# A diffusion backbone's opening in another order, with six smaller edits along its length

## The chip, the core and the metric

The kernel runs on one core of one Trainium2 chip. That core has a matrix engine (PE, whose weight loads the profile shows as PEld), a vector engine (DVE), an activation engine (ACT), a general engine (POOL), and the SP engine, which here only issues DMA. Matrix products accumulate in eight banks of PSUM, 512 columns of 32 bits each; all other tiles lie in SBUF. The metric is the device time of one execution in microseconds (us), the median over runs. Three runs of the kernel before took 2201.84, 2202.66 and 2203.73 us.

## The reference

Two layers of a hybrid backbone over 512 latent tokens and 256 context tokens, width 1024, all in 32-bit floats. Each layer does this:

```
m  = silu(cond) @ ada_w + ada_b          # six vectors per stream: shift, scale, gate, twice
h  = rms_norm(x) * norm_g * (1 + scale) + shift
u  = h @ w_in                            # one projection: keys, values, queries, pool columns, gate logits
A  = (mean over windows 2,4,8,16 of u_pool - u_pool) @ pool_w * pool_scale
B  = neighbourhood attention (4 heads, 8 x 16 window, bias na_rpb, plus all context keys)
C  = windowed attention with sinks;  D = latent attention with low-rank queries and keys
x += gate1 * (sum_i sigmoid(logits_i) * (branch_i @ w_branch_i)) @ w_out
x += gate2 * swiglu(rms_norm(x) * norm_g2 * (1 + scale2) + shift2)
```

The context tokens use the same weights with their own modulation vectors. In the second layer they give keys and values only. A last `rms_norm` gives the output. The modulation of layer 0 stands before everything else, because `h` needs its shift and scale.

## The kernel before

**Numbers.** A product of two 32-bit matrices is made of three fast ones: each operand is split into a high part (rounded by a copy on ACT, `act_copy` L142) and a low part (the difference, by DVE or POOL), and `mm3` (L148) adds high x high, low x high and high x low. `split_w` (L154) does so for weights; the low part goes to the engine named in `cur["lo"]`. A whole 32-bit product is also possible; the chip runs it as two PE instructions.

**Order of the work.** `Stream` (L36) holds a queue of jobs. A job has a load part, which issues the weights' DMAs and their split, and a run part. When a job starts, the next job's load part is traced too, so weights come one job ahead. A run part yields after each few products with the time it thinks they take, and small pieces of work can be deferred by such a time (`st.defer`) or asked for at once (`st.need`). `drive` feeds jobs between the steps of an attention. Instructions on PE, DVE, ACT and POOL are then placed in each engine's queue by a planner, which goes by the traced order and by its own estimate of when each is ready; SP alone keeps the traced order. A tile's tag has a fixed number of buffers, so an instruction that fills a buffer waits for the last reader of what it held. Raw weights have three such buffers, split ones four. PSUM has three banks under the tag `mm`, two under `sc`, two under `tr` and one under `pv`.

**Opening of layer 0.** SP issues x (twelve tiles), then 32 tiles of 256 KB of the first modulation: four groups of eight (shift and scale for chunks 0 to 3, then for 4 to 7). `ada_start` (L309) runs them as steps: the 16 of the first two groups are whole 32-bit products with the two conditioning columns `cs32`; the other 16 are split, with four columns `csp` (two high, two low), their high part by ACT or, each fourth, by DVE, and their low part by DVE (L328). `ada_run(n)` advances n yields, ten to a group. Meanwhile x is transposed chunk by chunk (`turn_xn` L606). `start_h` (L614) makes one chunk of `h`: for the 512 latent and 256 context columns DVE scales (L617), ACT adds the shift and rounds (L620), DVE makes the low part (L621). Chunks 0 to 3 follow the second group.

**First stage of layer 0**, in `mix` (L1312). First come the token-major rows (`tm_jobs` L656: values and small keys, eight jobs, one for each chunk of `h`, with six accumulators of 416 columns in six banks); the first four jobs alternate with the rest of the modulation. Then the mask load and the biases for the first two heads (`na_bias` L1013: a load and three adds each on POOL), chunks 4 to 7 of `h`, two jobs of pool columns (`pool_job` L716), the first queries (`na_q_job` L993, split by `split_q` L973) and the first keys (L1002, split by `split_k` L959). Each of these three kinds runs all eight chunks for the latent columns and then for the context columns, and leaves its accumulator by a post: the pool post copies it by ACT, adds shifted copies on DVE (L753), and defers a small product with `pool_w` by 20 us. Then neighbourhood attention starts; gate jobs (`gate_job` L798) and the next queries fill its waits. The rows go through DRAM (`vst`) to become attention's values. SP also stores x to DRAM (`xst`, eight stores), after the rows.

**First stage of layer 1.** The mask and the biases come first, then pool columns, first queries, the rows, the first keys, and attention.

**Seams later on.** `side_on` (L1426) and `side_one` (L1434) are jobs without a load part and without products. The first stands ahead of the fourth branch's gate jobs, the second ahead of the output projection; the latter loads the last two chunks of x and finishes two groups of the later modulation. That modulation (`ada_rest` L362) loads its own weights through SP while the products run. In the output projection and the last feed-forward product, `project_jobs` (L1444) runs the latent columns of all blocks before the context columns of the last four, defers `stats` by 2.0 us and `apply` by 5.5 us: sums of squares by PE, a Newton iteration on DVE (`newton` L439), `rstd_diag` (L475) with one diagonal matrix of 128 x 128 for each 128 tokens on DVE (L484), then their spread over rows by PE and the next `h`, chunk by chunk.

**The end.** `final_jobs` (L1607) adds the last products to x, squares on ACT, joins the halves' sums, runs `newton_col` (L455) on one column and scales the rows.

## Time and profile before

| what | value |
|---|---|
| median of three runs | 2202.66 us |
| lowest and highest | 2201.84, 2203.73 us |
| time of the profiled execution | 2204.7 us |
| its span, first to last instruction | 2202.9 us |
| mean granted clock of PE | 0.99 |
| busy: PE, DVE, ACT, POOL | 2136.4, 1252.0, 878.2, 715.4 us |

All rows come from the one profiled execution. Times in them count from the start of its span. "Busy" is the time in which an engine has an instruction under way; matrix products are pipelined, so their lengths overlap. An instruction is named by its line, engine and operation, then by what it writes and reads (`out<-in`) and the shapes. What stands in brackets is the time its engine was idle before it and what ended that. The granted clock is 1.00 at 2.4 GHz and 0.50 at 1.2 GHz; a value between is a mean over the stretch.

### The profile page before, as it was taken

Reading aid. Unit: us, or ns where it says so; the run is one execution under the profiler, and the core shown is the slowest. Engines: PE = TensorE matmul, PEld = TensorE weight load, DVE = VectorE, ACT = ScalarE, POOL = GpSimd, SP = SyncE. Lnnn points to the kernel's source line nnn. Section 1 sums busy time; section 2 is a strip of 40 time slices with the busy share of each in tenths; the row PEclk is TensorE's granted clock in tenths of the full one; section 3 lists DMA queues with packets and bytes.
Section 4 is the critical chain, followed back from the end, with each engine's and each line's share of the span. In section 5 each row is a group of like instructions: output and inputs, shape, how many; then the busy total and the mean of one; then the engine's idle time right before and its main releaser. Section 6 shows DMA issues by size and latency. Waiting matters only on the chain.

```text
span 2202.9 us, 32481 instructions
## 1 busy us (share of the span) xinstructions
PE 2136.4 (97%) x11796; PEld 1835.6 (83%) x11796; DVE 1252.0 (57%) x2804; ACT 878.2 (40%) x1967; POOL 715.4 (32%) x593
## 2 busy tenths in 40 slices
PE   7999999999999999999999989999999999999998
PEld 3888888888887898888888868887878898888886
DVE  6764667866799797555522264667776435212225
ACT  4454455544422322122122324555655434323233
POOL 1232222222223233333233322433233343444443
PEclk9999999999999999999999999999999999999999
DMA  7522122111356154444422223322222332333332
GB/s 253 155 73 53 44 51 53 42 41 51 121 174 188 48 168 138 139 143 152 142 66 62 87 79 92 99 66 63 57 68 66 91 111 82 100 96 93 105 96 91
DMA packets 316373, 214.74 MB, mean 97 GB/s; under 512 B 17434, under 2 KB 281908, under 8 KB 316212
## 3 DMA queue, kind: packets, MB, share of 16 engines
q1 hardware_dynamic: 307796, 204.79, 32.0%
q10 hardware_dynamic: 8416, 7.87, 1.1%
q8 instruction: 93, 1.52, 0.3%
q14 instruction: 68, 0.56, 0.1%
HBM read 202.90 MB, written 9.70 MB: 97 GB/s over the span
## 4 chain that ended last, share of the span: by engine, by line
PE 86%; DVE 6%; ACT 2%; issue 2%; DMA 2%; POOL 1%; SPq 0%; ACTq 0%; DVEq 0%; POOLq 0%
PE ps_w L149 13%; PE ps_w L150 13%; PE ps_w L151 13%; PE ps_gate L149 6%; PE ps_gate L150 6%; PE ps_gate L151 6%; PE pv L885 3%; PE tr L871 2%; PE ps_wo L151 2%; PE ps_wo L149 2%; PE ps_wo L150 2%; PE ps_y L149 2%; PE ps_y L151 1%; PE ps_y L150 1%; PE sc L934 1%
## 5 line engine op out<-in xcount | busy, mean ns | idle before, releaser
L157 POOL TENSOR_TENSOR gatelo<-gater,gatehi 128x512 fp32r<-128x512 f32 x128 | 172.9, 1353 | 427.9 <-ACT gatehi L143 412.6
L149 PE MATMUL ps_gate<-hh,gatehi 128*128 128x512 f32 (+1 forms) x768 | 277.9, 362 | 0.0
L150 PE MATMUL ps_gate<-hl,gatehi 128*128 128x512 f32 (+1 forms) x768 | 273.4, 356 | 0.0
L151 PE MATMUL ps_gate<-hh,gatelo 128*128 128x512 f32 (+1 forms) x768 | 272.9, 355 | 0.0
L400 DVE SCALAR_TENSOR_TENSOR adaacc<-adaraw,cs,adaacc 128x512 f32<-128x512 f32 x224 | 160.5, 749 | 86.1 <-DMA adaraw<-in_ada_w_dram 85.0
L149 PE MATMUL ps_w<-hh,w1hi 128*128 128x512 f32 (+1 forms) x480 | 170.8, 356 | 0.0
L149 PE MATMUL ps_w<-hh,w3hi 128*128 128x512 f32 (+1 forms) x480 | 170.3, 355 | 0.0
L150 PE MATMUL ps_w<-hl,w1hi 128*128 128x512 f32 (+1 forms) x480 | 170.0, 354 | 0.0
L150 PE MATMUL ps_w<-hl,w3hi 128*128 128x512 f32 (+1 forms) x480 | 170.0, 354 | 0.0
L151 PE MATMUL ps_w<-hh,w1lo 128*128 128x512 f32 (+1 forms) x480 | 169.8, 354 | 0.0
L151 PE MATMUL ps_w<-hh,w3lo 128*128 128x512 f32 (+1 forms) x480 | 169.8, 354 | 0.0
L157 POOL TENSOR_TENSOR w1lo<-w1r,w1hi 128x512 fp32r<-128x512 f32 x80 | 103.8, 1298 | 198.8 <-ACT w1hi L143 196.8
L149 PE MATMUL ps_w<-gh,w2hi 128*128 128x512 f32 (+1 forms) x472 | 165.6, 351 | 0.0
L151 PE MATMUL ps_w<-gh,w2lo 128*128 128x512 f32 (+1 forms) x472 | 165.4, 350 | 0.0
L150 PE MATMUL ps_w<-gl,w2hi 128*128 128x512 f32 (+1 forms) x472 | 165.2, 350 | 0.0
L157 POOL TENSOR_TENSOR w3lo<-w3r,w3hi 128x512 fp32r<-128x512 f32 x80 | 105.4, 1324 | 178.7 <-ACT w3hi L143 164.7
L151 PEld LDWEIGHTS ps_gate<-hh,gatelo 128*128 128x128 f32 x768 | 145.1, 189 | 19.7
L149 PEld LDWEIGHTS ps_gate<-hh,gatehi 128*128 128x128 f32 x768 | 145.3, 189 | 17.5
L150 PEld LDWEIGHTS ps_gate<-hl,gatehi 128*128 128x128 f32 x768 | 145.4, 189 | 16.6
L157 POOL TENSOR_TENSOR w2lo<-w2r,w2hi 128x512 fp32r<-128x512 f32 (+1 forms) x80 | 97.4, 1225 | 158.0 <-ACT w2hi L143 156.5
L1510 DVE SCALAR_TENSOR_TENSOR ft<-ft,ps_w 128x512 f32<-128x512 f32 (+1 forms) x68 | 39.6, 582 | 143.8 <-ACT ft L1509 143.6
L143 ACT ACTIVATE gatehi<-gater 128x512 fp32r<-128x512 f32 x128 | 80.3, 630 | 81.7 <-PE ps_gate L150 39.9
(419 smaller groups left out, 5599.2 us busy)
## 6 DMA issues: line engine op xcount, KB each, us to landing
adaraw<-in_ada_w_dram SPq DMA_DIRECT2D x160, 256.0 KB, 4.0
gater<-in_w_in_dram SPq DMA_DIRECT2D x128, 256.0 KB, 2.8
w1r<-in_ffn_w_dram SPq DMA_DIRECT2D x80, 256.0 KB, 2.9
w3r<-in_ffn_w_dram SPq DMA_DIRECT2D x80, 256.0 KB, 2.9
w2r<-in_ffn_w_dram SPq DMA_DIRECT2D x56, 256.0 KB, 2.8
ada<-in_ada_w_dram SPq DMA_DIRECT2D x32, 256.0 KB, 5.4
wbr<-in_w_branch_dram SPq DMA_DIRECT2D x64, 128.0 KB, 2.5
wor<-in_w_out_dram SPq DMA_DIRECT2D x32, 256.0 KB, 3.7
```

Source lines behind the costliest of these rows:

```text
L143: nc.scalar.activation(out=o, in_=i, func=AF.Copy, scale=scale)
L149: nc.tensor.matmul(ps, ah, bh, start=start, stop=False)
L150: nc.tensor.matmul(ps, ah, bl, start=False, stop=False)
L151: return nc.tensor.matmul(ps, al, bh, start=False, stop=stop).ins
L157: cur["lo"].tensor_tensor(out=lo, in0=raw, in1=hi.bitcast(F32), op=ALU.subtract)
L400: nc.vector.scalar_tensor_tensor(out=acc[j], in0=raw, scalar=c, in1=acc[j], op0=ALU.mult, op1=ALU.add)
L871: nc.tensor.transpose(tr[:, 128 * j:128 * j + 128], ps[qi][0][:, c0:c0 + 128], ident)
L885: nc.tensor.matmul(acc[:, 128 * q0:128 * (q0 + nq)], v[rows], t[rows, c:c + 128 * nq], start=(i == 0), stop=(i == nmm - 1))
L934: nc.tensor.matmul(ps, q[:, c0:c0 + 128], kd[:, k0:k0 + n], start=True, stop=False)
L1510: nc.vector.scalar_tensor_tensor(out=t, in0=t, scalar=1.0, in1=p1, op0=ALU.add, op1=ALU.mult)
```

## The change

It has seven parts. (1) The modulation steps of the first four groups alternate: even ones are whole, odd ones are split; ACT makes every high part; the low parts of the first two groups go to POOL, those of the last two to DVE. (2) Layer 0's first stage starts with both pool columns and the first queries together, as two jobs: chunks 0 to 3 of all three, then chunks 4 to 7; then come the rows, then the keys. The three raw weight tiles that SP loads among the first modulation weights belong to them. (3) The mask load, the stores of x and the biases of the first two heads move behind the opening or the rows, the biases in layer 1 too; a gate job asks for the pool columns after its first product. (4) The rows' six accumulators take their banks in another order. (5) `newton` leaves its result in SBUF, and the diagonals are made by ACT. (6) The jobs `side_on` and `side_one` go; the latter's work runs at the start of the first block of the output projection, and `apply` is deferred by 8.0 us there in layer 0. (7) At the end one instruction scales and joins the halves' sums.

```diff
-    cs32 = cp.tile([128, KD, 2], F32, name="cs32")
+    cs32 = cp.tile([128, KD, 4], F32, name="cs32")
...
-        nc.vector.tensor_copy(cs32, src)
+        nc.vector.memset(cs32[:, :, 2:4], 0.0)
+        nc.vector.tensor_copy(cs32[:, :, 0:2], src)
...
-            raw = ada0[i]
-            if i < 16:
-                w[i] = raw
-                return
-            w[i] = [rp.tile([128, 512], F32R, tag=t, name="ada" + t, bufs=3) for t in ("ph", "pl")]
-            if i % 4 == 3:
-                nc.vector.tensor_copy(w[i][0], raw)
-            else:
-                act_copy(w[i][0], raw)
-            nc.vector.tensor_tensor(out=w[i][1], in0=raw, in1=w[i][0].bitcast(F32), op=ALU.subtract)
-        for i in range(4):
+            raw = w[i] = ada0[i]
+            if i % 2:
+                hi, lo = w[i] = [rp.tile([128, 512], F32R, tag=t, name="ada" + t, bufs=3) for t in ("ph", "pl")]
+                act_copy(hi, raw)
+                (nc.gpsimd if i < 16 else nc.vector).tensor_tensor(out=lo, in0=raw, in1=hi.bitcast(F32), op=ALU.subtract)
+        for i in range(5):
...
-            if n == 2:
-                nc.tensor.matmul(ps[0:2, :], cs32[:, k, :], wi, start=(k == 0), stop=(k == KD - 1))
+            if i % 2 == 0:
+                nc.tensor.matmul(ps[0:4, :], cs32[:, k, :], wi, start=(k == 0), stop=(k == KD - 1))
...
-        g = t
+        g, res = t, y
...
-            V.scalar_tensor_tensor(out=y, in0=t, scalar=1.5, in1=y, op0=ALU.add, op1=ALU.mult)
-        return y
+            V.scalar_tensor_tensor(out=res if i == 2 else y, in0=t, scalar=1.5, in1=y, op0=ALU.add, op1=ALU.mult)
+        return res
...
-            i = nc.vector.tensor_scalar(out=dg[:, 128 * t:128 * t + 128], in0=ident, scalar1=r[:, 2 * t:2 * t + 1], scalar2=None, op0=ALU.mult)
+            i = nc.scalar.activation(out=dg[:, 128 * t:128 * t + 128], in_=ident, func=AF.Copy, scale=r[:, 2 * t:2 * t + 1])
...
+    OPEN = (O_POOL, O_POOL + 128, O_NA_Q)
+    open0 = []
+    def open_raw(i):
+        raw = wp.tile([128, 4, 128], F32, tag="wraw", name="openr", bufs=3)
+        r0, c0 = 512 * (i // 3), OPEN[i % 3]
+        nc.sync.dma_start(raw, a["w_in"][0][r0:r0 + 512, c0:c0 + 128].rearrange("(k p) c -> p k c", p=128))
+        return raw
...
         if i in (13, 15, 17):
-            raw = wp.tile([128, 416], F32, tag="wraw", name="tmr", bufs=3)
-            load_tm(raw, 0, len(tm0))
-            tm0.append(raw)
+            open0.append(open_raw(len(open0)))
...
-                    ps.extend(psum(("mm", "mm", "mm", "sc", "sc", "tr" if last else "pv")[t], "ps_tm", 416) for t in range(6))
+                    ps.extend(psum(tag, "ps_tm", 416) for tag in ("tr", "mm", "mm", "sc", "mm", "sc"))
...
                 if i == 0 and m == 0:
-                    st.need("pool0", "pool1", "xst")
+                    st.need("xst")
...
                     yield from mm_piece(pg, w[0], cur["h"], (s0, s1))
+                    if i == 0 and m == 0:
+                        st.need("pool0", "pool1")
...
+        def opening_jobs(ys):
+            posts = [pool_job(i, ys)[1] for i in range(2)]
+            q, ps = [], []
+            def post_q(p_, piece):
+                if not q:
+                    q.extend(new_q())
+                split_q(p_, piece, q, True)
+            posts.append(post_q)
+            def load(half):
+                out = []
+                for i in range(3):
+                    raw = open_raw(3 + i) if half else open0[i]
+                    tiles = [big("y", [128, 4, 128], F32R, "open" + t) for t in ("hi", "lo")] if i < 2 else None
+                    out.append(split_w(raw, [128, 4, 128], "open", tiles))
+                return out
+            def product(i, k, w):
+                for p_, (s0, s1) in zip(ps[i], (PL, PC)):
+                    hh, hl = cur["h"][k]
+                    cur["pe"] = mm3(p_, w[i][0][:, k % 4, :], w[i][1][:, k % 4, :], hh[:, s0:s1], hl[:, s0:s1], k == 0, k == KD - 1)
+            def run(half, w):
+                if half == 0:
+                    ps.extend((psum("mm", "ps_open"), psum(tag, "ps_open", 256)) for tag in ("sc", "sc", "pv"))
+                for k in range(4 * half, 4 + 2 * half):
+                    for i in range(3):
+                        product(i, k, w)
+                    yield 9 * NT / 2400
+                if half:
+                    for i in range(3):
+                        for k in (6, 7):
+                            product(i, k, w)
+                        for p_, piece in zip(ps[i], (PL, PC)):
+                            posts[i](p_, piece)
+                        yield 6 * NT / 2400
+            return [st.add(lambda w, h=h: run(h, w), lambda h=h: load(h)) for h in range(2)][1], q
...
             def first_biases():
-                nc.sync.dma_start(nam, a["k_namask"])
                 bias.extend(na_bias(e, nam) for e in range(2))
             def after_tm():
...
-                if not last:
-                    for k in range(KD):
-                        st.defer(2.0 + 4.0 * k, lambda k=k: nc.sync.dma_start(xst[k], xn[k]), "xst")
             if not last:
                 cur["lo"] = nc.vector
+                jo, q0 = opening_jobs(y_pool)
                 tm = tm_jobs()
+                jk, k0 = na_k_job(0)
                 for k in range(4):
-                    ada_run((6, 7, 7, 0)[k])
-                    st.until(tm[k], False)
-                nam = big("c", [128, 3, 32, 8], F32, "nam")
-                first_biases()
+                    ada_run(5)
+                    st.step()
                 for k in range(4, KD):
                     start_h(k)
-                jobs = pool_jobs(y_pool)
-                jq0, q0 = na_q_job(0)
-                jk, k0 = na_k_job(0)
+                st.until(jo, False)
+                nam = big("c", [128, 3, 32, 8], F32, "nam")
+                nc.sync.dma_start(nam, a["k_namask"])
+                for k in range(KD):
+                    st.defer(4.0 + 3.0 * k, lambda k=k: nc.sync.dma_start(xst[k], xn[k]), "xst")
                 st.until(tm[-1], False)
                 after_tm()
-                st.until(jobs[1], False)
             else:
                 nam = big("c", [128, 3, 32, 8], F32, "nam")
-                first_biases()
+                nc.sync.dma_start(nam, a["k_namask"])
...
             jq1, q1 = na_q_job(1)
+            first_biases()
             st.until(jk, False)
...
-        def side_on(_):
-            return
-            yield
-        st.add(side_on)
...
-        def side_one(_):
+        def last_turns():
             turn_x(KD - 2)
             st.defer(6.0, lambda: turn_x(KD - 1), "x")
             if not last:
                 ada_until(2)
-            return
-            yield
-        st.add(side_one)
...
+                if b == 16 and m == 0:
+                    last_turns()
...
-                    st.defer(5.5, apply, "norm")
+                    st.defer(8.0 if b == 16 and not last else 5.5, apply, "norm")
...
-                    o = 8 if i else 2 * t + j
+                    o = 2 * t + j + i
                     nc.scalar.activation(out=p[:, c], in_=x[:, c], func=AF.Square, accum_out=ssq[:, o:o + 1])
-                if len(parts) > 1:
-                    nc.vector.tensor_tensor(out=ssq[:, 7:8], in0=ssq[:, 7:8], in1=ssq[:, 8:9], op=ALU.add)
+                    if j:
+                        v = ssq[:, o:o + 1]
+                        nc.vector.tensor_scalar(out=v, in0=v, scalar1=1.0 / D, scalar2=ssq[:, o - 1:o], op0=ALU.mult, op1=ALU.add)
...
-                v = ssq[:, 2 * t + 1:2 * t + 2]
-                nc.vector.scalar_tensor_tensor(out=v, in0=v, scalar=1.0 / D, in1=ssq[:, 2 * t:2 * t + 1], op0=ALU.mult, op1=ALU.add)
-                r = newton_col(v)
+                o = 2 * t + 1 + t // 3
+                r = newton_col(ssq[:, o:o + 1])
```

## Rows read from the trace of the kernel before

**Rows 1.** The page, part 1: busy us, share of the span, instructions.

```profile
PE 2136.4 (97%) x11796; PEld 1835.6 (83%) x11796; DVE 1252.0 (57%) x2804; ACT 878.2 (40%) x1967; POOL 715.4 (32%) x593
```

**Rows 2.** Busy time by stretch: length, PE, PEld, DVE, ACT, POOL, clock, DMA share.

```profile
16.00:33.00 17.00, 17.00 (x52) 3.98 (x50) 6.06 (x23) 2.88 (x6) 0.00 (x0) 1.00 0.99 338
33.00:71.00 38.00, 32.00 (x146) 22.48 (x145) 34.85 (x72) 20.46 (x38) 6.39 (x6) 0.96 0.38 119
114.00:131.00 17.00, 12.46 (x55) 9.92 (x54) 10.02 (x27) 10.72 (x26) 4.13 (x4) 0.80 0.26 64
16.00:131.00 115.00, 103.97 (x487) 74.84 (x486) 79.94 (x191) 52.83 (x107) 21.89 (x18) 0.96 0.55 172
```

**Rows 3.** Chain of waits, 16 to 62 us: start, length, what.

```profile
16.19 6.96 PE ps_ada L341 x16
57.37 0.24 PE ps_ada L343
```

**Rows 4.** DVE groups by line, 33 to 71 us: busy, mean ns, idle before.

```profile
L328 DVE TENSOR_TENSOR adapl<-ada,adaph 128x512 fp32r<-128x512 f32 x16 | 12.7, 823 | 0.1
L617 DVE SCALAR_TENSOR_TENSOR nh<-xn,mod,rrow 128x512 f32<-128x512 f32 (+1 forms) x16 | 9.3, 614 | 0.1
L621 DVE SCALAR_TENSOR_TENSOR hl<-nh,mod,hh 128x512 fp32r<-128x512 f32 (+1 forms) x15 | 8.8, 623 | 0.0
L157 DVE TENSOR_TENSOR tmlo<-tmr,tmhi 128x416 fp32r<-128x416 f32 x5 | 2.9, 582 | 0.0
L325 DVE CAST adaph<-ada 128x512 fp32r<-128x512 f32 x4 | 2.1, 524 | 0.0
L600 DVE TENSOR_SCALAR dg<-ident,nwy 128x128 f32<-128x128 f32 x6 | 1.4, 280 | 0.0
```

**Rows 5.** Timeline of DVE in the opening: start, length, instruction.

```profile
34.54 0.69 DVE L328 TENSOR_TENSOR adapl<-ada,adaph 128x512 fp32r<-128x512 f32 x1
54.49 3.04 DVE L328 TENSOR_TENSOR adapl<-ada,adaph 128x512 fp32r<-128x512 f32 x3
```

**Rows 6.** Timeline of POOL in the opening.

```profile
49.99 6.39 POOL L1024 TENSOR_TENSOR bias<-braw,nam 128x192 f32<-128x192 f32 x6 [48.68 <-DMA braw<-in_k_rpb_dram]
```

**Rows 7.** Busy time by stretch, seams of layer 1.

```profile
1335.00:1345.00 10.00, 8.11 (x35) 7.61 (x35) 3.31 (x9) 2.52 (x5) 2.20 (x3) 0.83 0.18 47
1380.00:1385.00 5.00, 2.98 (x16) 2.11 (x16) 4.79 (x13) 2.93 (x9) 2.67 (x3) 1.00 0.46 112
```

**Rows 8.** Timeline of the SP queue before the output projection.

```profile
655.12 10.59 SPq L373 DMA_DIRECT2D adaraw<-in_ada_w_dram  x6
665.80 0.94 SPq L163 DMA_DIRECT2D wor<-in_w_out_dram  x2
```

**Rows 9.** Busy time by stretch, start of the output projection, layer 0.

```profile
665.00:680.00 15.00, 10.84 (x45) 8.43 (x44) 13.05 (x22) 3.73 (x7) 5.53 (x4) 0.77 0.80 238
```

**Rows 10.** Busy time by stretch, start of the output projection, layer 1.

```profile
1775.00:1785.00 10.00, 7.94 (x51) 7.53 (x51) 2.32 (x3) 3.21 (x6) 4.76 (x4) 0.83 0.38 109
```

**Rows 11.** Timeline: diagonals on DVE, and a 128 x 128 pass on ACT.

```profile
736.42 3.02 DVE L484 TENSOR_SCALAR dg<-ident,ps_ssq 128x128 f32<-128x128 f32 x4
...
104.73 0.30 ACT L143 ACTIVATE pwh<-pwr 128x128 fp32r<-128x128 f32 x1
```

**Rows 12.** Busy time by stretch, second norm of layer 0.

```profile
735.00:745.00 10.00, 7.96 (x49) 7.28 (x48) 8.17 (x15) 4.36 (x9) 5.14 (x4) 0.83 0.52 160
```

**Rows 13.** Timeline of DVE at the end.

```profile
2195.47 1.13 DVE L1655 SCALAR_TENSOR_TENSOR ssq<-ssq 128x1 f32<-128x1 f32 x1
```

**Rows 14.** Timeline: first pool add, last query split, and PE after it.

```profile
88.13 2.42 DVE L753 TENSOR_TENSOR pb<-pb 128x527 f32<-128x527 f32 x2 [4.45 <-ACT pb L143]
...
112.27 0.43 DVE L984 SCALAR_TENSOR_TENSOR q<-ps_naq,q 64x256 fp32r<-64x256 f32 x1
...
118.76 0.38 PE L149 MATMUL ps_pw<-yph,pwh 128*128 128x256 f32 x1 [3.89 <-DVE ypl L779]
```

More of the change, by code (lines that the diff above doesn't have):

```diff
@@ L333, in ada_start @@
         for i, (b0, k) in enumerate(steps):
-            prepare(i + 4)
+            prepare(i + 5)
             if k == 0:
                 ps = psum("tr", "ps_ada")
-            wi = w.pop(i)
-            n = 2 if i < 16 else 4
-            if n == 2:
-                nc.tensor.matmul(ps[0:2, :], cs32[:, k, :], wi, start=(k == 0), stop=(k == KD - 1))
+            wi = w[i]
+            if i % 2 == 0:
+                nc.tensor.matmul(ps[0:4, :], cs32[:, k, :], wi, start=(k == 0), stop=(k == KD - 1))
             else:
@@ L346, in ada_start @@
             if k == KD - 1:
-                row = tmp([n, 512], F32, "adar")
-                act_copy(row, ps[0:n, :])
+                row = tmp([4, 512], F32, "adar")
+                act_copy(row, ps[0:4, :])
                 yield
-                ps2 = psum("tr", "ps_adat", 4 * n)
+                ps2 = psum("tr", "ps_adat", 16)
                 for j in range(4):
-                    nc.tensor.transpose(ps2[:, n * j:n * j + n], row[:, 128 * j:128 * j + 128], ident[:n, :n])
-                if n == 2:
-                    ada_cols(0, b0, ps2.rearrange("p (j c) -> p j c", c=2), 2)
-                    yield
-                    continue
+                    nc.tensor.transpose(ps2[:, 4 * j:4 * j + 4], row[:, 128 * j:128 * j + 128], ident[:4, :4])
                 red = cp.tile([128, 4, 2], F32, tag="adared", name="adared", bufs=1)
@@ L448, in newton @@
         V.tensor_scalar(out=y.bitcast(I32), in0=g.bitcast(I32), scalar1=-1, scalar2=0x5F3759DF, op0=ALU.mult, op1=ALU.add)
-        for _ in range(3):
+        for i in range(3):
             V.scalar_tensor_tensor(out=t, in0=y, scalar=-0.5, in1=v, op0=ALU.mult, op1=ALU.mult)
             V.tensor_tensor(out=t, in0=t, in1=y, op=ALU.mult)
-            V.scalar_tensor_tensor(out=y, in0=t, scalar=1.5, in1=y, op0=ALU.add, op1=ALU.mult)
-        return y
+            V.scalar_tensor_tensor(out=res if i == 2 else y, in0=t, scalar=1.5, in1=y, op0=ALU.add, op1=ALU.mult)
+        return res
     def newton_col(v):
@@ L540, in transposed @@
         return ps
-    tm0 = []
+    OPEN = (O_POOL, O_POOL + 128, O_NA_Q)
[5 more added lines that the diff above has]
+        return raw
     def load_tm(raw, l, k):
@@ L659, in load @@
             def load(k):
-                if l == 0 and k < len(tm0):
-                    raw = tm0[k]
-                else:
-                    raw = wp.tile([128, 416], F32, tag="wraw", name="tmr", bufs=3)
-                    load_tm(raw, l, k)
+                raw = wp.tile([128, 416], F32, tag="wraw", name="tmr", bufs=3)
+                load_tm(raw, l, k)
                 return split_w(raw, [128, 416], "tm")
@@ L1309, in mla_heads @@
             return heads
+        def opening_jobs(ys):
[25 more added lines that the diff above has]
+                if half:
+                    for i in range(3):
+                        for k in (6, 7):
[4 more added lines that the diff above has]
+            return [st.add(lambda w, h=h: run(h, w), lambda h=h: load(h)) for h in range(2)][1], q
         def mix():
@@ L1438, in side_one @@
                 ada_until(2)
-            return
-            yield
-        st.add(side_one)
         def project_jobs(w, name, h_, b, new_norm, first, rest, r0=0, kn=KD):
```

## The prediction

> **What bounds the kernel now.** I read the page's busy times first, then busy time by stretch, then groups by line, the chain and the timeline where PE stood idle. PE is busy for 97% of the span [rows 1], so only its idle and slow-clocked time can be won back, or an end that no PE work covers. By stretch, 16 to 131 us holds 103.97 us of PE busy in 115 at a mean granted clock of 0.96 [rows 2]: 11.0 us idle, and 0.04 x 115 = 4.6 us lost to the lower of its two levels (1.2 instead of 2.4 GHz), 15.6 in all. From 16 to 33 PE is full and the DMA share is 0.99. From 33 to 71 DVE is the bound: 34.85 of 38 us. From 114 to 131 PE stands 4.5 us and loses 0.20 x 17 = 3.4 to the clock [rows 2]: the first attention waits for keys and pooled columns. Small holes of the same kind lie at 665, 735, 1335, 1380 and 1775 us, and the end is a serial DVE chain.
>
> **The modulation steps.** A whole step is two PE instructions: sixteen of them take 6.96 us, 0.87 a step. A split step is two of 0.24, 0.48 [rows 3]. Before, 16 steps are whole and then 16 split; after, each pair has one of each. PE's total is unchanged, 8 x 0.39 = 3.1 us of it moves from the first two groups to the last two. The wider stationary operand (4 columns, two of zeros) I cost at nothing: the split steps already use 4 columns at 0.24. DVE keeps 8 of 16 low parts and no copy. Eight low parts go to POOL, idle from 16 to 33 [rows 2]; ACT makes all 16 high parts, with 2.9 of 17 us used there.
>
> **DVE in 33 to 71.** Its load now: low parts 12.7, the scaled chunks 9.3 and 8.8, token-major low parts 2.9, copies 2.1, diagonals 1.4 [rows 4]. Low parts cost 0.69 alone, but 3.04 for three while POOL adds the biases from 49.99 for 6.39 us [rows 5, 6]. Those adds leave this stretch. After: 8 x 0.69 = 5.5 (7.2 less), no copies (2.1 less), and for five token-major splits the six of 512 columns, 6 x 0.69 = 4.1 (1.2 more): 34.85 - 8.1 = 26.8 us. Beside it PE has 8 x 0.87 + 8 x 0.48 = 10.8 us of modulation and four chunks of the opening, each 9 x 0.24 + 9 x 0.12 = 3.2 us, 12.9 together. With 23.7 us against 26.8 the two nearly match; chunks 4 to 7 then come at some 2.4 us each from DVE (9.3 + 8.8 for 7.75 chunks [rows 4]) against 3.2 us of PE. PE becomes the bound.
>
> **The new order.** Pooled columns, first queries, token-major rows and first keys are the same PE work. Their posts (pool chains, query split) now run under eight token-major chunks instead of beside first attention. SP issues three 256 KB loads early instead of three times three small ones, three more after the late rows' loads, then the token-major ones; the eight stores of x now go out in that stage. I cost these issues at nothing, since PE has the first half to run; if SP is held up there, the second half is late by that. The pool need, moved behind the first gate product, removes a wait; the mask load is covered by the same stage. Layer 1 of the kernel already runs pool, queries, rows, keys in this order, so it prices the seams: entering the rows it loses 10 - 8.11 = 1.9 idle and 0.17 x 10 = 1.7 clock, and entering attention 2.0 idle at full clock [rows 7]. Left over of the 15.6: 2.0 for attention, 1.8 (half of 3.6, because the one bank that waits for the query split is now asked for fifth and not third), and 2 for the first two groups, which now run at the pace of landing weights, since DMA is already full there [rows 2]. The opening gains 15.6 - 5.8 = 9.8 (bounds: 0 and 15.6). The same bank order gains 0.7 at layer 1's rows (0 to 3.6).
>
> **The stub before the output projection.** SP issues its first weights at 665.80 because it first sat in the six modulation loads queued at 655.12, for 10.59 us [rows 8]. Without the stub they are issued one gate job earlier, ahead of those loads, with some ten us to land and be split. The stretch 665 to 680 loses 15 - 10.84 = 4.2 idle and 0.23 x 15 = 3.5 clock [rows 9]. Next late is the last merged chunk, used eighth by the first product. I take 6.5 of 7.6 (bounds 0 to 7.6). In layer 1 the same seam loses 10 - 7.94 = 2.1 and 1.7 [rows 10]; its weights do land in time and PE waits for a merged chunk that ACT takes behind a weight copy. With SP's order changed I take 1.5 (0 to 3.8). The other stub I cost at nothing: no hole stands there.
>
> **Diagonals on ACT.** At 736.42 four cost DVE 3.02 us; a 128 x 128 pass costs ACT 0.30 [rows 11], so 1.2. But this edit also sends the normalisation 2.5 us later down PE's stream, so its chunks start about when they do now. Of the 10 - 7.96 = 2.0 idle and 1.7 clock there [rows 12] I take 1.0 (0 to 3.7). Elsewhere (queries' and keys' norms, layer 1's first norm) DVE is freed of the same work: 1.1 together, an estimate from 0.75 a piece under POOL (0 to 3). Behind ACT's new passes wait its exponentials, by 0.6 to 1.2 us, under PE work.
>
> By the Trainium skill, SBUF — State Buffer, section "SBUF: two separate sides", DVE with a two-port mode or two SBUF inputs and a reading GpSimd lock each other out for a whole instruction, and ACT waits for neither. The trace agrees: 0.28 a diagonal in the opening, 0.75 at 736 with POOL 5.1 us busy in ten [rows 4, 11, 12]. By that rule the eight POOL parts could hold the first Newton chain, nine such instructions, by some 9 x 1.3 = 12 us at most (estimate); it has that room, since the diagonals run after 33 [rows 4].
>
> **Biases.** Their 6.39 us of POOL [rows 6] come, in both layers, between the last rows and attention, with weights' low parts. I take 1.5 lost in layer 1 (0 to 6.4); in layer 0 the 2 us of leftover stand for it.
>
> **The end.** On one-element columns, an add and then a multiply-add; the latter takes 1.13 us beside POOL [rows 13]. One instruction replaces both: 1.1 gained (0.2 to 1.3).
>
> Sum: 9.8 + 0.7 + 6.5 + 1.5 + 1.0 + 1.1 - 1.5 + 1.1 = 20.2 us, or 20. Against the profiled execution (span 2202.9, time 2204.7) that is a span of 2183 and a time of 2185; its time is 2.0 above the median 2202.66, so the median forecast is 2183.
>
> **Rivals.** First: the opening gives nothing, because weights, not DVE, set when chunks 4 to 7 start. For it: DMA share 0.99 from 16 to 33 [rows 2]. Against: 0.38 afterwards, while DVE is full. Only the seams gain: 2183 + 10 = 2193.
>
> Second: the bias adds land in front of keys' casts and the next weights' low parts, and each attention starts a POOL pass later: 2 x 6.4 less the 1.5 counted = 11, so 2194. For it: those adds had POOL to themselves before, and the seam in layer 1 already stands 2.0 us [rows 7]; against: attention has other products to run. The Trainium skill's lock (same section) would add waits of the casts here; no row shows them.
>
> Third, slower: DVE's queue at the first row. The opening holds six banks; the query bank is free only after its split, and if that stands behind both pool chains, PE stops. The chain from the first pool add to the last query split ran from 88.13 to 112.70, 24.6 us [rows 14]. All of it exposed, with 3.4 of clock as after the 3.89 us hole [rows 2, 14], is 28: 2183 - 1.8 + 28 = 2209. It turns into a loss from some 20 us exposed. Against it: POOL no longer slows these adds, and other banks can run on.
>
> Fourth: all holes close fully (15.6, 7.6, 3.6, 3.7, 3.8 and the rest): some 2167.
>
> **How the numbers follow.** Forecast 0.55 (its own range 2177 to 2189), first 0.16, second 0.12, third 0.07, fourth 0.10. What a measurement of this kernel tells from no change is about 0.2%, 4.4 us. Parts of the first two (0.07) end within it, so faster 0.86, same 0.07, slower 0.07. The range 2170 to 2196 takes in the first two and leaves out the third and most of the fourth.
>
> **What would show it.** Right: PE busy above 108 of the 115 us after 16; DVE's last scaled chunk before 62; the first projection weights issued near 655 and no hole there; diagonals as ACT passes of 0.3; one DVE instruction before the last Newton chain. Wrong: PE idle over 5 us where the rows start or attention starts, POOL bias adds ending after the first scores, or a longer hole at 1380. If the span falls by under 10, the opening step has failed.

## The result

The changed kernel takes 2180.34 us (median of 4 runs, 2177.47 to 2181.39) against 2203.19 us for the kernel before, run beside it: ratio 0.9894, 95% interval 0.9877 to 0.9911. The forecast was 2183 in 2170 to 2196. The profiled execution took 2180.71 us with a span of 2178.9, which is 24.0 shorter than that of before. The total came out as forecast; where it came from did not.

The page, part 1, of the changed kernel: PE is busy for 9 us less than in [rows 1], DVE for 22 us less.

```profile
PE 2127.5 (98%) x11796; PEld 1826.5 (84%) x11796; DVE 1229.6 (56%) x2763; ACT 890.5 (41%) x2009; POOL 712.6 (33%) x595
```

To see where the time went, the same product is looked up in both traces. Each line of this table is the start of one PE product (the last two: the end of PE's work and the span), before and after; the last column is what the stage that ends there gained.

```
product                                  before    after   ahead by   of this stage
first gate product, layer 0               135.1    128.2      6.9        6.9
last gate products before the projection  659.1    651.4      7.7        0.8
output projection, late                   729.0    718.7     10.3        2.6
feed-forward, early                       753.8    741.2     12.6        2.3
feed-forward, end                        1292.8   1280.4     12.4       -0.2
layer 1, within the rows                 1345.1   1322.1     23.0       10.6
layer 1, first gates                     1394.6   1375.0     19.6       -3.4
layer 1, last before the projection      1772.3   1752.7     19.6        0.0
layer 1, output projection               1792.0   1768.5     23.5        3.9
end of PE's work                         2193.8   2170.9     22.9       -0.6
span                                     2202.9   2178.9     24.0        1.1
```

Not all of this can be read to the microsecond: the changed kernel and the ninth and eleventh runs below have the same instructions in the same order through all of layer 0, and their last gate products before the projection start at 651.4, 650.8 and 652.3, 1.5 us apart. In the kernel before it is more: runs 1, 2, 3 and 5 below share its order through the opening, and the first gate products of these five lie between 132.6 and 135.3, 134.4 on average. Those of the changed kernel and of runs 8, 9, 11 and 12, the same in the opening, lie between 127.7 and 128.5, 128.0 on average. So the opening is better put at 6.4 us than at 6.9.

**The opening.** Busy time by stretch in the changed kernel (columns as in [rows 2]):

```profile
16.00:33.00 17.00, 14.84 (x52) 3.82 (x52) 14.09 (x26) 7.42 (x14) 10.87 (x8) 1.00 1.07 371
33.00:71.00 38.00, 37.70 (x178) 23.56 (x179) 29.60 (x66) 20.20 (x38) 0.00 (x0) 1.00 0.46 144
...
107.00:124.00 17.00, 14.92 (x77) 12.48 (x76) 7.66 (x24) 10.33 (x24) 10.40 (x11) 0.90 0.63 173
16.00:131.00 115.00, 109.57 (x534) 79.21 (x535) 79.44 (x200) 57.92 (x119) 23.53 (x22) 0.99 0.54 171
```

PE is now full from 33 to 71, and idle for 2.2 us in the first stretch, where it was full before [rows 2]. Idle and clock loss in 16 to 131 fell from 15.6 to 5.4 + 1.2 = 6.6 us, in a stretch that now reaches 7 us further into the work. The first keys start only 1.6 us earlier than before, the first gate product 6.9: most of the gain lies where attention starts. DVE's timeline there (start, length, instruction, idle before):

```profile
58.74 0.17 DVE L348 TENSOR_REDUCE adared<-ps_adat 128x8 f32<-128x16 f32 x1 [2.54 <-PE ps_adat L346]
...
67.04 0.48 DVE L613 SCALAR_TENSOR_TENSOR nh<-xn,mod,rrow 128x256 f32<-128x256 f32 x1
```

DVE waits for PE at 58.74: PE has become the bound, as forecast, but so the last scaled chunk comes at 67, not before 62.

**The projection of layer 0.** SP's queue and PE's waits in the changed kernel:

```profile
642.29 0.93 SPq L163 DMA_DIRECT2D wor<-in_w_out_dram  x2
...
647.37 10.79 SPq L363 DMA_DIRECT2D adaraw<-in_ada_w_dram  x6
```

```profile
667.58 0.38 PE L369 MATMUL ps_ada<-adapart,quads 128*128 128x32 f32 x2 [0.93 <-DVE adapart L398]
685.87 0.38 PE L369 MATMUL ps_ada<-adapart,quads 128*128 128x32 f32 x2 [1.14 <-DVE adapart L398]
701.03 0.50 PE L149 MATMUL ps_wo<-mhh,wohi 128*128 128x512 f32 x1 [0.91 <-ACT wohi L143]
702.39 0.50 PE L151 MATMUL ps_wo<-mhh,wolo 128*128 128x512 f32 x1 [0.62 <-POOL wolo L157]
```

The first weights are now issued at 642.29, ahead of the six modulation loads [rows 8], and the seam of [rows 9] is gone: 32 products in, PE is 15.0 us ahead. But four waits follow, 3.6 us of idle in all and 4.7 by the starts of the products; the first two are for sums of the later modulation, the others for weights. 10.3 is left.

**The opening of layer 1** gained most, and no step of the prediction was about it. Both kernels: PE at the product with ones over the context columns (`ps_ssq` x4), then the SP queue with the biases' raw tiles (`braw`) and the raw pool weights (`poolr`), and the pool weights' high part on ACT. Before:

```profile
1311.52 0.99 PE L480 MATMUL ps_ssq<-ones,acc 128*128 128x2 f32 x4 [7.97 <-DVE acc L473]
1312.37 0.77 PE L149 MATMUL ps_pool<-hh,poolhi 128*128 128x512 f32 x1
```

```profile
1288.06 5.66 SPq L1017 DMA_DIRECT2D braw<-in_k_rpb_dram  x2
1293.82 20.22 SPq L163 DMA_DIRECT2D poolr<-in_w_in_dram  x4
...
1311.67 1.66 ACT L143 ACTIVATE poolhi<-poolr 128x512 fp32r<-128x512 f32 x3
...
1312.36 3.74 POOL L157 TENSOR_TENSOR poollo<-poolr,poolhi 128x512 fp32r<-128x512 f32 x3 [13.46 <-ACT poolhi L143]
```

After:

```profile
1291.47 0.50 PE L150 MATMUL ps_pool<-hl,poolhi 128*128 128x512 f32 x1 [0.77 <-DVE hl L511]
...
1294.78 0.50 PE L470 MATMUL ps_ssq<-ones,acc 128*128 128x2 f32 x4
```

```profile
1254.88 27.04 SPq L163 DMA_DIRECT2D poolr<-in_w_in_dram  x4
...
1279.55 0.61 ACT L143 ACTIVATE poolhi<-poolr 128x512 fp32r<-128x512 f32 x1
...
1280.25 2.53 POOL L157 TENSOR_TENSOR poollo<-poolr,poolhi 128x512 fp32r<-128x512 f32 x2 [19.31 <-ACT poolhi L143]
```

Before, PE came to that product first, and its operand, a sum on DVE, stood behind the scaling of the latent chunks in DVE's queue. The pool products that follow could not have filled the hole either: ACT rounded their weights only from 1311.67, after the latent chunks. POOL was not what held them up, since it had done the adds by 1298.9 and then stood idle for 13.46 us until that rounding. What came late is the raw weights, and SP's waits show why (who waited for whom: us in total, times, longest):

```profile
SPq L1017 <- DVE acc L473: 21.4, 1, 21.4
```

The first bias load waited 21.4 us for a buffer, one of seven that it shares with the squares of the norm, until DVE (L473) had added one of these; the second waited 4.9 us more. The pool weights stood behind both in SP's queue, which keeps the traced order. In the changed kernel the first of their loads is issued at 1254.88, their rounding on ACT stands ahead of the latent chunks, and the product with ones stands behind pool products and waits for nothing. Busy time by stretch shows what that hole cost, idle and clock; before, then after:

```profile
1300.00:1320.00 20.00, 11.52 (x51) 8.77 (x50) 16.81 (x41) 9.45 (x17) 6.27 (x5) 0.74 0.18 43
```

```profile
1287.00:1307.00 20.00, 19.23 (x93) 15.41 (x93) 17.90 (x42) 10.93 (x21) 5.70 (x5) 1.00 0.22 58
```

**The start of attention.** The bias adds on POOL and busy time around layer 1's first scores, after:

```profile
112.20 2.13 POOL L1019 TENSOR_TENSOR bias<-braw,nam 128x192 f32<-128x192 f32 x3 [1.30 <-DVE k L966]
...
1346.09 4.57 POOL L1019 TENSOR_TENSOR bias<-braw,nam 128x192 f32<-128x192 f32 x6 [9.99 <-DMA braw<-in_k_rpb_dram]
```

```profile
1345.00:1368.00 23.00, 19.29 (x97) 15.64 (x96) 15.36 (x37) 15.11 (x35) 14.26 (x14) 0.93 0.59 155
```

In layer 0 they end at 114.3, after the first scores at 112.5, and in layer 1 at 1350.7, after the first scores at 1349.7: one of the signs named as wrong, in both layers. In layer 1 the next queries' and gates' low parts stand behind them (PE waits 0.81 us for one at 1352.47), and the stage gives back 3.4 us. Not all of that is theirs: run 9 below, which has no adds there, gives back 1.2.

**Layer 1's projection and the end.** Busy time at the seam of [rows 10], and the one instruction that replaces the add and the multiply-add of [rows 13]:

```profile
1752.00:1762.00 10.00, 10.00 (x79) 9.61 (x78) 3.04 (x5) 3.42 (x7) 3.88 (x3) 1.00 0.36 109
```

```profile
2172.38 0.21 DVE L1662 TENSOR_SCALAR ssq<-ssq 128x1 f32<-128x1 f32 x1 [0.19 <-ACT fp L1659]
```

### The profile page after: what moved, and what is told of

Its sections match the earlier page's. It is cut to its first block, busy times and chain, and to the rows that moved or that the text cites. A ratio compares the mean times of both kernels' runs of the same rounds, so it can differ in the third digit from the quotient of the medians.

```text
span 2178.9 us, 32494 instructions
## 1 busy us (share of the span) xinstructions
PE 2127.5 (98%) x11796; PEld 1826.5 (84%) x11796; DVE 1229.6 (56%) x2763; ACT 890.5 (41%) x2009; POOL 712.6 (33%) x595
## 4 chain that ended last, share of the span: by engine, by line
PE 85%; DVE 7%; ACT 3%; DMA 2%; issue 2%; POOL 1%; SPq 0%; ACTq 0%; DVEq 0%; POOLq 0%
PE ps_w L149 13%; PE ps_w L150 13%; PE ps_w L151 13%; PE ps_gate L149 6%; PE ps_gate L150 6%; PE ps_gate L151 6%; PE pv L880 3%; PE tr L866 3%; PE ps_y L149 2%; PE ps_y L151 1%; PE ps_y L150 1%; PE ps_wo L151 1%; PE ps_wo L150 1%; PE ps_wo L149 1%; DVE adaacc L390 1%
## 5 line engine op out<-in xcount | busy, mean ns | idle before, releaser
L157 POOL TENSOR_TENSOR w3lo<-w3r,w3hi 128x512 fp32r<-128x512 f32 x80 | 105.1, 1320 | 174.9 <-ACT w3hi L143 173.4
## 6 DMA issues: line engine op xcount, KB each, us to landing
wbr<-in_w_branch_dram SPq DMA_DIRECT2D x64, 128.0 KB, 2.3
```

The costliest lines, as they stand in the source:

```text
L157: cur["lo"].tensor_tensor(out=lo, in0=raw, in1=hi.bitcast(F32), op=ALU.subtract)
```

## The experiments

The experiments are told in the order of the argument; the numbers are those of the runs. The theory that they set out from: layer 1's opening gained because its biases no longer stand ahead of the pool weights (theory A, which put it down to the adds in POOL's queue); the rival is that the diagonals on ACT closed that hole. Ratios are against the kernel before, with their 95% interval; 0.001 is 2.2 us.

**1. Only layer 1's biases later.**

```diff
                 nam = big("c", [128, 3, 32, 8], F32, "nam")
-                first_biases()
+                nc.sync.dma_start(nam, a["k_namask"])
...
             jq1, q1 = na_q_job(1)
+            if last:
+                bias.extend(na_bias(e, nam) for e in range(2))
```

> The kernel before, with one edit: in layer 1 the loads and adds of the first two heads' biases come after the rows instead of before the pool columns. Theory A (the bias adds, by where they stand in POOL's queue, put the context columns' product with ones ahead of the pool products): that product moves behind pool products, PE's hole of 7.97 us at 1303.55 is gone, the layer-1 rows start some 11 us earlier, and 3 to 4 of that are given back where layer-1 attention starts. The whole is 6.5 to 8.5 us faster than before. Theory B (the diagonals on ACT closed that hole): the hole stays, and the whole is 0 to 2 us slower.

Measured: 2193.28 us, ratio 0.9957 (0.9943 to 0.9972), 9.5 us faster. The stretch that answers to 1300 to 1320:

```profile
1298.00:1318.00 20.00, 19.12 (x95) 15.67 (x96) 18.11 (x38) 9.77 (x18) 5.38 (x6) 1.00 0.25 65
```

The hole is gone by this move alone. SP issues the first raw pool weight at 1266.53 and not at 1293.82, and ACT starts to round it at 1291.13 and not at 1311.67; the mask load stayed where it was, so it is not what held SP. Less is given back at the attention than expected (12.6 us ahead in the rows, 10.5 at the first gates), hence 9.5 and not 6.5 to 8.5.

**2. Only the Newton result in SBUF and the diagonals on ACT** (the edits of `newton` and `rstd_diag` in the diff, nothing else).

> The kernel before, with two edits of one part: the Newton result goes to SBUF and the diagonals are made by ACT. Theory A (bias order): the hole of 7.97 us at 1303.55 stays within 1.5 us of its length, and the whole is 0.5 to 2.5 us faster, from the norms of queries and keys and the two norms over a layer. Theory B (diagonals): the hole is gone and the whole is some 9 to 11 us faster.

Measured: 2199.59 us, 0.9983 (0.9974 to 0.9992), 3.7 us faster.

```profile
1305.58 0.98 PE L480 MATMUL ps_ssq<-ones,acc 128*128 128x2 f32 x4 [8.32 <-DVE acc L473]
```

The hole stays: the rival falls. The gain is at layer 0's second norm, 3.9 us there, more than theory A gave for the whole.

**9. The mirror: the changed kernel with layer 1's biases back.**

```diff
                 nc.sync.dma_start(nam, a["k_namask"])
+                first_biases()
                 jobs = pool_jobs(y_pool)
...
             jq1, q1 = na_q_job(1)
-            first_biases()
+            if not last:
+                first_biases()
```

> The changed kernel, with layer 1's first two biases back where they stood, ahead of its pool columns; the mirror of the first experiment. Theory A (that move alone gave some 11 us at layer 1's opening and cost 2 to 3.4 where its attention starts): a wait of 6 to 9 us ahead of the context columns' product with ones is back, and the whole is 7 to 11 us slower than the changed kernel, so 11 to 15 faster than before. Theory B (the diagonals and the earlier normalisation would close the hole without it): the hole is under 3 us and the whole within 3 us of the changed kernel.

Measured: 2189.64 us, 0.9939 (0.9925 to 0.9953), 13.4 us faster than before; the changed kernel's own ratio gives 23.3, so the move back costs 9.9 (the two profiled spans differ by 7.9).

```profile
1299.33 0.99 PE L470 MATMUL ps_ssq<-ones,acc 128*128 128x2 f32 x4 [8.31 <-DVE acc L463]
```

The hole is back at its old length, and with it SP's wait of 21.4 us; the first raw pool weight is issued at 1281.95, against 1254.88 in the changed kernel. The move of two biases in layer 1 is worth about 10 of the 23 us; everything the prediction counted as a gain comes to some 13. Loads and adds moved together in every run, so no run separates them. The five traces read for this (before, runs 2 and 9 with the wait, run 1 and the changed kernel without) speak for the loads in SP's queue and against the adds: POOL stands idle for 13.1 to 13.5 us in front of the low parts in each trace with the hole. Why the planner then puts the rounding on ACT behind the latent chunks when the weights come late is inferred, not shown.

**3. Only the two stubs out.** The edit is the removal of `side_on` and `side_one` and the call of `last_turns` as in the diff.

> The kernel before, with the two jobs without products taken out and their work put at the start of the output projection's first block; nothing else. Theory A (the stubs alone make both seams): layer 0's projection starts 4 us earlier, gains 7 at most and gives 1 to 3 back to waits for the later modulation's sums; layer 1's gains some 3.8; the whole is 8 to 10 us faster. Rival: layer 1's seam gained because the work before it had moved, not by the stubs: then 4.5 to 6 us faster. If the waits for the modulation's sums came from the stubs' removal, PE shows waits for adapart of about 1 us each in this run too.

Measured: 2197.4 us, 0.9976 (0.9968 to 0.9985), 5.3 us faster. Layer 1's seam gains its 3.8 by the stubs alone. Layer 0's projection starts 3.9 us earlier against the work ahead of it, is 7.3 ahead after some 30 products, and keeps 2.1: with one wait of 1.44 us for adapart, two of 0.33 and 0.63 for weights, and a clock of 0.83 from 670 to 680. So theory A has the place right and layer 0's price wrong; the rival's total fits for another reason.

**6. The modulation's sums one gate job earlier, in the changed kernel.**

```diff
-            if m == 1 and not last:
+            if m == 0 and not last:
                 cur["side"] = 1.4
```

> The changed kernel, with the later modulation's steps starting one gate job earlier (at the fourth branch's first gate job instead of its second). Theory A (layer 0's output projection is paced by DVE's modulation sums once the stub is gone: DVE is busy for 97% of it and PE waits for adapart): the two waits of 0.93 and 1.14 us go, and the whole is 2 to 4 us faster than the changed kernel. Theory B (PE's holes there come from the weights' loads behind the modulation's loads, or the sums then delay the merged chunks): within 1 us of the changed kernel, or up to 3 us slower.

Measured: 2184.8 us, 0.9914 (0.9900 to 0.9927), some 4.4 slower than the changed kernel. The gate products ahead of the projection, this run and then the changed kernel:

```profile
635.00:655.00 20.00, 17.42 (x100) 15.21 (x99) 19.88 (x36) 6.76 (x14) 7.05 (x6) 0.91 0.62 190
```

```profile
635.00:655.00 20.00, 20.00 (x115) 17.57 (x114) 19.43 (x36) 6.46 (x13) 6.43 (x5) 1.00 0.56 178
```

DVE is full there already. The wait for adapart moved ahead, to 2.58 us at 642, and the gate products there lose more than the projection wins. The sums fill DVE from 635 on wherever they start. That they pace the projection was not shown by taking them away; that starting them one job earlier doesn't help was.

**4. The changed kernel with the old modulation steps** (`prepare` and the loop of `ada_start` as before: 16 whole, 16 split on DVE).

> The changed kernel, with the modulation steps of before: 16 whole, then 16 split with all low parts and four copies on DVE. Theory A (the mixed steps take 7.6 us off DVE between 33 and 71 us, and that lets PE be the bound there): DVE is busy for over 35 of the 38 us again, the first keys come 3 to 6 us later than in the changed kernel, and the whole is 17 to 20 us faster than before. Rival B (the new order alone did it, since the opening gives PE other work while DVE catches up): within 1 us of the changed kernel, that is 22 to 23 us faster than before. Rival C (the first groups go at the pace of landing weights, so that whole steps there are free and split ones later are cheap): up to 2 us faster than the changed kernel.

Measured: 2181.14 us, 0.9904 (0.9888 to 0.9921).

```profile
16.00:33.00 17.00, 16.77 (x52) 4.18 (x52) 6.92 (x27) 4.25 (x8) 0.00 (x0) 1.00 1.07 373
33.00:71.00 38.00, 35.78 (x180) 24.32 (x179) 34.38 (x77) 21.90 (x39) 0.00 (x0) 1.00 0.49 153
```

DVE is as busy as before (34.4 of 38 us), yet PE stands only 2.2 us instead of 6.0: the new order alone does that, since PE has the opening's chunks to run. The mixed steps close the other 1.9 and pay 1.9 in 16 to 33. First keys come 1.7 us later without them, but the total is not told apart from the changed kernel's. That is rival B, nearly.

**5. Only the pool need behind the first gate product.**

```diff
-                    st.need("pool0", "pool1", "xst")
+                    st.need("xst")
...
                     yield from mm_piece(pg, w[0], cur["h"], (s0, s1))
+                    if i == 0 and m == 0:
+                        st.need("pool0", "pool1")
```

> The kernel before, with one line moved: the first gate job asks for the pool columns after its first product and not ahead of it. Theory A (the hole of 4.57 us where attention starts in layer 0 comes from that line alone, and the new order of the opening is not needed for it): the gate's product, 24 passes of 0.23 us, covers the wait; the hole and the lower clock behind it go, and the whole is 4 to 7 us faster than before. Theory B (the pool chains on DVE are late by more than that, because they run beside the keys and queries): PE waits a little later, at the same or at another product, and the whole is 0 to 2 us faster. By A most of what the opening gained is this line; by B it is the order.

Measured: 2204.3 us, 1.0002 (0.9993 to 1.0011): nothing.

```profile
120.25 0.58 PE L149 MATMUL ps_pw<-yph,pwh 128*128 128x256 f32 x1 [4.53 <-DVE ypl L779]
```

PE still waits for the pool columns' low part, at a product that does not go by the need. The edit in fact moved nothing: every engine's queue, SP's too, holds the same instructions in the same order as before, so the line alone is not what gained. The DVE pass that PE waits for (L779) starts at 118.0 before; with the new order its first is at 96.6, and that hole is gone. That the opening's gain at attention is the order's rests on run 4 above: with the new order and the old steps, the first gate product is 5.6 us ahead.

**12 and 8. Diagonals on DVE again; the deferral of 5.5 again**, each in the changed kernel (the lines of the diff undone: `newton` and `rstd_diag` in one, `st.defer(5.5, apply, "norm")` in the other).

> The changed kernel, with the Newton result left in PSUM and the diagonals made by DVE as before. Theory A (the diagonals are worth what they gave alone, 4.8 us, of which 2 to 4 at the normalisation ahead of layer 0's feed-forward part): 3 to 5 us slower than the changed kernel, a wait for the diagonals of 1.5 us or more there or the chunks later by as much. Theory B (as the prediction has it: 1.0 there and 1.1 elsewhere, the deferral of 8.0 hides the rest): 0 to 2 us slower.

> The changed kernel, with the normalisation behind layer 0's output projection deferred by 5.5 us as before, not by 8.0. Theory A (with the diagonals early, 8.0 holds the normalisation back): the first feed-forward products start some 1 to 1.5 us earlier, and the whole is 1 to 1.5 us faster than the changed kernel. Theory B (as the prediction has it, 8.0 only keeps PE from waiting for the diagonals): a hole of 0.5 to 1.5 us ahead of the spread over rows, and the whole is equal or up to 2 us slower.

Measured: 2180.66 us, 0.9896 (0.9882 to 0.9910), and 2180.51 us, 0.9894 (0.9880 to 0.9907); neither differs from the changed kernel. The 16 us around the second norm, in order: neither edit (run 3), later deferral alone (12), ACT alone (8), and both (the changed kernel):

```profile
732.00:748.00 16.00, 13.96 (x76) 11.98 (x76) 14.44 (x25) 7.62 (x15) 6.49 (x6) 0.89 0.27 84
```

```profile
727.00:743.00 16.00, 15.08 (x94) 12.83 (x93) 14.13 (x28) 8.75 (x16) 7.75 (x6) 1.00 0.36 106
```

```profile
725.00:741.00 16.00, 16.00 (x98) 13.83 (x97) 13.22 (x27) 10.38 (x21) 7.92 (x6) 1.00 0.37 113
```

```profile
724.00:740.00 16.00, 15.22 (x94) 12.80 (x93) 12.02 (x25) 10.14 (x20) 7.67 (x6) 1.00 0.35 107
```

Either edit removes the wait for the diagonals (2.04 us) and the low clock behind it. Together they are worth no more than one; the deferral even costs 0.8 idle once ACT makes the diagonals. From the late projection to the early feed-forward products, run 3 gains nothing on the kernel before, the deferral alone 2.3, ACT alone 4.0, and both 2.3. Undoing one shows nothing, though doing it alone showed 3.9 at this place: two cures for one wait.

**7, 10 and 11. The biases among the rows.** In both layers after the fourth rows job (7); in layer 0 after the seventh and in layer 1 after the sixth (10); in layer 1 alone after the sixth (11). The edit of 10:

```diff
+                st.until(tm[6], False)
+                first_biases()
                 st.until(tm[-1], False)
...
+                st.until(tm[5], False)
+                first_biases()
                 st.until(tm[-1], False)
...
             jq1, q1 = na_q_job(1)
-            first_biases()
```

> The changed kernel, with the biases of the first two heads loaded and added among the rows (after the fourth rows job) instead of after them, in both layers. Theory A (in layer 1, 3.4 us are lost where attention starts because POOL adds biases for 4.6 us just ahead of the next queries' and gates' low parts): POOL is free there, layer 1's first scores come 1 to 3 us earlier, layer 0's up to 2 us; the whole is 1 to 5 us faster than the changed kernel. Theory B (attention itself sets that start, by keys and DVE): within 1 us of it. Theory C (the adds hold the rows' low parts on POOL in layer 1 and slow DVE's splits in layer 0): up to 3 us slower.

> The changed kernel, with the first two heads' biases loaded and added among the rows, after the seventh rows job in layer 0 and after the sixth in layer 1 (the run before had them after the fourth, where the adds met the query split in layer 0 and the context's normalisation in layer 1). Theory A (POOL must be free where attention starts and DVE must not be slowed where the rows start): both attention starts keep what the run before showed (PE busy some 15.8 of 17 us and 21.5 of 23 us there), and the rows start as in the changed kernel; 3 to 6 us faster than the changed kernel. Theory B (the adds cost as much wherever they stand): within 1 us of it.

> The changed kernel, with the biases among the rows in layer 1 alone (after the sixth rows job). Theory A (POOL's adds ahead of the next queries' and gates' low parts cost layer 1's attention start 3.4 us): 2 to 4 us faster than the changed kernel, all of it between layer 1's rows and its first gates. Theory B: within 1 us of it.

Measured: 2181.37 us, 0.9904 (0.9889 to 0.9919); 2178.79 us, 0.9888 (0.9874 to 0.9902); 2180.29 us, 0.9899 (0.9885 to 0.9913). Both attention starts in run 10:

```profile
107.00:124.00 17.00, 15.91 (x92) 13.01 (x91) 10.06 (x29) 11.10 (x26) 6.69 (x6) 1.00 0.56 165
1345.00:1368.00 23.00, 21.50 (x122) 18.17 (x121) 16.39 (x43) 18.51 (x45) 12.06 (x10) 1.00 0.49 130
```

PE gains 1.0 and 2.2 busy us and full clock at the two places. But where the rows start, DVE's passes up to the query split now run beside POOL's adds, and PE waits for the split, in run 7 (layer 0), in run 10 and in run 11 (layer 1):

```profile
81.36 0.43 PE L149 MATMUL ps_tm<-tmhi,hh 128*128 128x416 f32 x1 [3.20 <-DVE q L979]
```

```profile
1322.12 0.43 PE L149 MATMUL ps_tm<-tmhi,hh 128*128 128x416 f32 x1 [1.42 <-DVE q L979]
```

```profile
1325.37 0.43 PE L149 MATMUL ps_tm<-tmhi,hh 128*128 128x416 f32 x1 [1.91 <-DVE q L979]
```

In the changed kernel that wait is 0.69 us in layer 0 and absent in layer 1. What attention gains, the rows give back. Run 10 has the lowest median of all, 1.6 us under the changed kernel, but their intervals overlap: it is not shown to be better.

## Why the prediction was right, and where it was not

The time is right by luck: two errors of opposite sign cancelled. The prediction's own terms, without its bias term, summed to 21.7 us; run 9, which has all of them and leaves layer 1's biases where they were, gains 13.4. The move that was priced at a loss of 1.5 brought 9.9.

- **Biases.** This step failed. It said that the adds go to the start of attention and cost 1.5 (0 to 6.4) there. They do cost there: the stage gives back 3.4, of which some 2.2 are theirs (2.1 in run 1; 1.2 is given back without them in run 9). What it left out is what stood behind them at the old place: in SP's queue, behind bias loads that waited 21.4 us for a buffer, the raw pool weights, and at the end of that a wait of PE of 7.97 us with its clock. That hole is in the trace of before, but in none of the rows that the prediction worked from.
- **Modulation steps and DVE.** Said: 8.1 us less on DVE in 33 to 71 (34.85 to 26.8) makes PE the bound. DVE came down by 5.3, to 29.60. PE did become the bound, but run 4 shows it nearly so without that relief. The term was 9.8 for the whole opening; 6.4 to 6.9 came, 5.6 of it in run 4 too, by the order. The 2 us left over for the first two groups were measured at 2.2.
- **The stub.** Mechanism right (weights before the modulation's loads, no hole at the first product), size wrong: 6.5 forecast, 2.6 measured (1.5 and 2.2 in runs 9 and 11, the same there), 2.1 alone. "Next late" was not the last merged chunk, but DVE's sums, then weights; run 6 shows only that starting the sums earlier does not help. Layer 1, with no such sums, gave 3.9 against 1.5.
- **Diagonals.** 1.0 forecast at the second norm, 2.3 measured, and not by the diagonals alone: the deferral, said only to keep the chunks' start, removes the same wait. Elsewhere 1.1 forecast: run 2, with this edit alone, gains 3.7 in all and 3.9 at this norm, so nothing clear of the scatter is left for the other places.
- **Bank order.** 0.7 forecast, none found: the wait for the query split (1.89) is gone, and one for DVE's low part of the context columns (2.58 at 1315.8) has come in its place. That is not the banks' doing: run 9, with the new bank order and the biases at their old place, waits 1.88 for the split as before, and run 1, with the old order and the biases late, does not wait for it, but 1.23 for the low part.
- **The end.** 1.1 forecast, 1.1 measured.
- **The rivals.** The first (the opening gives nothing) falls; the second (attention waits a POOL pass longer) happened in part, in layer 1, at some 2.2 and not 11; the third (DVE's queue at the first row) shrank to a wait of 0.69 us; the fourth would need holes closed that stayed.

## What to carry to other kernels

A piece of work that is "off the path" can still hold up what another engine needs: here a small load at the head of the in-order SP queue waited 21.4 us for a buffer, and weights stood behind it. Before pricing a move, list what stands behind the moved work at its old place as well as at the new one, in the load queue too, and search the whole span for long waits of the bound engine that touch any queue involved. When two edits cure the same wait, undoing either shows nothing, and doing either alone shows its whole gain; only all four combinations tell. A seam that is closed can be paid back within the stage by the next late operands: here a lead of 15.0 us became 10.3.

## What the runs showed of the hardware

DVE beside POOL, in the changed kernel's first groups: Newton steps on 128 x 6 elements take 0.17 us until POOL's low parts start at 17.42, then about 1, and 0.17 again from 22.56, when POOL has stopped; a copy out of PSUM between them keeps its 0.41.

```profile
17.32 0.17 DVE L441 TENSOR_TENSOR nwt<-nwt,nwy 128x6 f32<-128x6 f32 x1
17.52 1.19 DVE L442 SCALAR_TENSOR_TENSOR nwy<-nwt,nwy 128x6 f32<-128x6 f32 x1
18.64 0.41 DVE L608 COPY xn<-ps_xt 128x256 f32<-128x256 f32 x1
...
20.21 0.98 DVE L441 TENSOR_TENSOR nwt<-nwt,nwy 128x6 f32<-128x6 f32 x1
```

```profile
17.42 5.08 POOL L324 TENSOR_TENSOR adapl<-ada,adaph 128x512 fp32r<-128x512 f32 x4 [16.12 <-ACT adaph L143]
```

This is what the Trainium skill, SBUF — State Buffer, section "SBUF: two separate sides", states: a DVE instruction with two SBUF inputs waits out a whole GpSimd instruction that reads SBUF. The trace agrees: some 0.8 to 1.0 us more on each of five such instructions (four Newton steps, and the modulation's add at 26.29 beside POOL's next low parts), against 1.27 for one low part on POOL. As the prediction expected, the chain had that room. Ahead of the query split DVE had none: in run 7 two passes on 128 x 8 elements (L755) take 0.80 us beside POOL's adds and 0.24 after them, and PE waits 1.4 to 3.2 us for the split in runs 7, 10 and 11. How much of these waits is this slowing and how much the new order of DVE's queue is not separated.
